# Half of a hybrid encoder layer's feed-forward by Strassen's seven products, its second matrix in three chunks

## The chip, the cores and the metric

The kernel runs on one core of one Trainium2 chip. A core has engines that run their own instruction queues side by side: TensorE (PE in the profile; PEld is its weight load) multiplies matrices into the accumulators (PSUM, eight banks), VectorE (DVE) and ScalarE (ACT) work on elements, SyncE (SP) issues most transfers. Semaphores hold an instruction until its data is there or its buffer is free; an engine's queue is in order, so an instruction that waits holds up all behind it.

The metric is the device time of one execution, in microseconds (us). Before the change it is 1327.59 us, the median of three runs (1327.44 to 1327.77).

## The reference, cut to what matters

Input is 512 tokens of 1024 features. 16 learned tokens are put in front (528 in all), and one layer follows: a feed-forward, a mixer of three branches (Fourier, short convolution, gated DeltaNet), and a second feed-forward. In front of each stands a norm, behind each another norm and the residual; the 16 tokens are dropped at the end. Everything is float32. The change is in both feed-forwards:

```python
def swiglu(x, wi, wo):
    a, b = jnp.split(x @ wi, 2, axis=-1)
    return (jax.nn.silu(a) * b) @ wo
...
h = h + 0.5 * rmsnorm(swiglu(rmsnorm(h, n[0]), ffn1_wi[l], ffn1_wo[l]), n[1])
```

`wi` is 1024 x 5632 and `wo` 2816 x 1024. In tiles of 128, x has 8 (`KD`), and the gated product 22 (`KF`). Tile m of a and tile m of b, columns m and 22 + m of `wi`, are the "tile pair" m.

## The kernel before, in words

**Layout.** Features lie on the 128 partitions and tokens on the free axis. The first feed-forward and the mixer's projections run over all 528 tokens, in two halves of 264 (`ALLC`), since a PSUM bank holds 512 numbers a partition; the second one over the 512 real tokens, whose halves of 256 fit one bank together (`REAL`, "joined").

**Numbers.** TensorE multiplies in float32r, which keeps 12 significant bits of an operand. So each operand is split into a high part h (a cast on ScalarE) and a low part l (a subtraction on VectorE), and each product is three passes: h x h, h x l, l x h. `mm` (the matmuls are issued on L137) does these three passes for one k. `load` fetches a tile of weights (1024 numbers a partition, 512 KB) on SP's queue to a staging tile `ws` (two buffers), casts it to `wh` (L219) and subtracts to `wl` (L220; three buffers each). `split` does the same for activations (L224, L225). `unit` is load, then `mm` over the 8 k: one tile of the first matrix.

**Order.** The order on TensorE is the order of the program. On the other engines a list scheduler sets it at build time, by priority (the place in the program) among what is ready; `load` is put 150 instructions ahead. Small side work of the norms and the mixer is put between the products by `side`, `tick` and `drain`.

**A feed-forward (`ffn`).** x has the gain of the norm in it, but not the root of the mean square: the first units run before this root (`rx`) is known. The three first tiles (a0, b0, a1) are begun in `start` or `edge`, three more follow, and meanwhile `xstat` has worked out `rx` (its last instructions are reciprocals on VectorE, L276). From then on each pair is: two units; each evicted from PSUM by VectorE with a multiplication by `rx` (`scaled`, L504); silu on ScalarE (L530); the product on VectorE (L526); and the split to tile m of `gh` and `gl`, which hold all 22 gated tiles. Then the second matrix: for each of the 8 output tiles, 22 k, whose weights come in three loads of 8, 8 and 6 tiles; `evict_y` copies the result to `ya`, squares it and adds up the squares for the norm.

**The edge.** The last output tile is left to the next stage (`tail`). `edge` does it half by half of the tokens (`part`), so that the norm, the residual and the next x of the first half go on while TensorE does the second half, and then begins the next stage's first three tiles. `finish` does the same at the end of the kernel, and writes the output.

Of the kernel before, what the change touches and what calls it, by code (L numbers as in the profile page):

```python
# [29 lines left out]
AHEAD = 150  # L30
XW = 5.0
# [23 lines left out]
# columns of the packed constants  # L55
# [45 lines left out]
class Cols:  # L101
    """Token columns of a stage, in two halves; joined: both fit one PSUM bank."""
# [17 lines left out]
class Tensor:  # L120
    """The tensor engine's instructions, with a sum of their length that orders the side work."""
# [22 lines left out]
class K:  # L144
# [43 lines left out]
    # side work goes between the large products; it yields how far on its next part goes  # L188
# [22 lines left out]
    # weights: staged as stored, then split into two parts of 12 significand bits  # L211
# [93 lines left out]
    def evict_y(self, ya, m, ps, gain=None, table=KD - 2):  # L305
        """ps: (half, what the products of tile m gave for it)"""
        y, acc = ya
        ACT, V = self.nc.scalar, self.nc.vector
        for i, p in ps:
            w = acc[i].shape[1]  # L310
            if gain is None:
                ACT.copy(y[i][:, m, :w], p)
            else:
                ACT.activation(y[i][:, m, :w], p, AF.Copy, scale=self.gains[:, gain, m:m + 1])
            if m == 0:
                ACT.activation(acc[i], p, AF.Square)
            else:
                sq = self.t(self.tp, "sy", [P, HN], F32, 1)[:, :w]
                ACT.activation(sq, p, AF.Square)  # L319
                V.tensor_tensor(acc[i], acc[i], sq, op=ALU.add)  # L320
        if m == table:
# [12 lines left out]
    def start(self, xT, gpre, srcs):  # L334
        """the first norm and tiles: everything arrives in the order of need"""
# [28 lines left out]
        # warm-up products while the first loads arrive  # L364
# [10 lines left out]
    def edge(self, C, hT, ya, gpost, gpre, tail, switch, nxt):  # L375
# [18 lines left out]
        tiles, tx, tc = tail()  # L394
        for t in tiles:
            self.evict_y(ya, t[0], [(0, self.part(t, tx, tc[0], W))], table=tiles[0][0] - 1)
# [12 lines left out]
        for t in tiles:  # L409
            self.evict_y(ya, t[0], [(1, self.part(t, tx, tc[1], W, lambda: next(e, None)))], table=-1)  # L410
# [20 lines left out]
    def finish(self, hT, ya, tail, out):  # L431
        """the last norm and residual; the second half of the tokens goes by tokens"""
# [5 lines left out]
        (tile,), tx, tc = tail()  # L438
        last = tile[0]
# [8 lines left out]
        self.evict_y(ya, last, [(0, self.part(tile, tx, tc[0], W))], 5, -1)  # L448
# [36 lines left out]
        p = self.part(tile, tx, tc[1], W, lambda: next(e, None))  # L485
# [3 lines left out]
        ACT.activation(sq[:, :W], p, AF.Square)  # L489
        ACT.activation(y[1][:, last, :W], p, AF.Copy, scale=self.gains[:, 5, last:last + 1])  # L490
# [20 lines left out]
    def open_ffn(self):  # L511
        ctx = ExitStack()
        gp = ctx.enter_context(self.tc.tile_pool(name=self.uid("gp"), bufs=1))
        self.gp = gp
        self.t3 = lambda: self.t(gp, "t3", [P, 530], F32, 3)
        return ctx

    def ffn(self, pre, wi, wo, C, gain=None):
        nc = self.nc
        x, os = pre  # L520
        gh = self.t(self.gp, "gh", [P, KF, L], F32R)
        gl = self.t(self.gp, "gl", [P, KF, L], F32R)
        u = C.u

        def pair(m, a, b):
            nc.vector.tensor_tensor(a[:, u], a[:, u], b[:, u], op=ALU.mult)  # L526
            self.split(gh[:, m, u], gl[:, m, u], a[:, u])

        def silu(a):
            nc.scalar.activation(a[:, u], a[:, u], AF.Silu)  # L530

        y = self.ytile().rearrange("p k c -> p (k c)")
        a, b, a1 = (y[:, i * L:(i + 1) * L] for i in range(3))
# [4 lines left out]
        for t in (a, b):  # L538
            nc.vector.tensor_tensor(t[:, u], t[:, u], self.rx[:, u], op=ALU.mult)
        silu(a)  # L540
        pair(0, a, b)
        nc.vector.tensor_tensor(a1[:, u], a1[:, u], self.rx[:, u], op=ALU.mult)
        silu(a1)
        b = self.t3()
        self.scaled(b, o)
        pair(1, a1, b)
        for m in range(2, KF):
            a = self.t3()
            self.scaled(a, o2 if m == 2 else self.unit(wi[m], x, C))
            silu(a)  # L550
            b = self.t3()
            self.scaled(b, o3 if m == 2 else self.unit(wi[KF + m], x, C))
            pair(m, a, b)
        ya = self.start_y(C)
        chunks = [(k0, min(8, KF - k0)) for k0 in range(0, KF, 8)]
        g = (gh, gl)
        for m in range(KD - 1):
            o = self.outs(C)
            for k0, n in chunks:
                w = self.load(wo[m][:, k0:k0 + n], n)  # L560
                for k in range(n):
                    self.mm(o.full, w, g, k, k0 + k, k0 + k == 0, k0 + k == KF - 1)
            self.evict_y(ya, m, [(i, p) for i, (p, _) in enumerate(o.half)], gain)

        def tail():
            ws = [(self.load(wo[KD - 1][:, k0:k0 + n], n), n, k0) for k0, n in chunks]
            return [(KD - 1, [(w, k, k0 + k) for w, n, k0 in ws for k in range(n)])], g, C.halves
        return ya, tail

# [18 lines left out]
    def mixer(self, pre, hT):  # L588
# [100 lines left out]
        def tail():  # L689
            ws = [(m, self.load(A["wout"][m])) for m in range(KD - NT, KD)]  # L690
            return [(m, [(w, k, k) for k in range(KD)]) for m, w in ws], (mh, ml), CS.halves
# [39 lines left out]
    def fold(self, q, o, fh, fl):  # L731
# [13 lines left out]
        def fold():  # L745
# [18 lines left out]
            # token L - k for k = 1 .. L/2 - 1  # L764
# [30 lines left out]
    # per-token scalars of both directions, [token, head, direction, tile]; tile 4: meta tokens  # L795
# [6 lines left out]
    def ab(self, ab):  # L802
# [23 lines left out]
        # softplus(a) = max(a, 0) + 2 atanh(e / (2 + e)), e = exp(-|a|)  # L826
# [5 lines left out]
        # beta = 1 / (1 + exp(-x))  # L832
# [50 lines left out]
    # short conv and silu of one head's q, k or v  # L883
# [8 lines left out]
    # token-major copies and l2norm  # L892
# [38 lines left out]
    # both heads' k: l2norm, token-major and back  # L931
# [41 lines left out]
    def rsqrt(self, dst, src, scale=1.0):  # L973
        """1 / sqrt(src * scale + eps) of a few columns: a first value from the exponent, then Newton's steps"""
# [11 lines left out]
    # chunk matrices and the scan of a pair of heads, both directions  # L986
    def dn_core(self, st, slack):
# [6 lines left out]
        # [token, head * 2 + direction, tile]  # L994
# [11 lines left out]
        # exponents gc_i - gc_j, masked  # L1006
# [36 lines left out]
        # inverses of the 32 x 32 diagonal blocks, one block a partition  # L1043
# [55 lines left out]
        # the blocks beside the diagonal  # L1099
# [25 lines left out]
        # scan  # L1125
# [80 lines left out]
    # gated norm of one head's output, back to channel-major, in place  # L1206
# [30 lines left out]
def body(tc, A):  # L1237
    nc = tc.nc
    with ExitStack() as ctx:
# [15 lines left out]
        ya, tail = k.ffn(pre, wi, wo, ALLC)  # L1255
# [14 lines left out]
        ya, tail = k.ffn(pre, wi, wo, REAL, 5)  # L1270
# [55 lines left out]
```

## Time and profile before

| | |
|---|---|
| median of three runs | 1327.59 us |
| the profiled execution: its span, from the first to the last instruction | 1325.0 us |
| TensorE: matmuls / weight loads, busy | 1311.5 us (99%) / 1159.8 us (88%) |
| VectorE / ScalarE, busy | 741.3 us (56%) / 492.3 us (37%) |
| first matrix of the first feed-forward, tile pair 2 on | about 37 to 266 us |
| its second matrix | 266 to 395 us |
| mixer, from the first to the second edge | 395 to 940 us |
| first matrix of the second feed-forward, tile pair 2 on, to the end of its second matrix | about 974 to 1319 us |
| read from HBM, written | 116.42 MB, 5.28 MB |

"Busy" is the time in which an engine has an instruction in work. Matmuls are pipelined: one of 264 columns is shown as 0.28 us long while the next one starts 0.12 us later, so what a stage costs is read from the distance of starts. A line such as `L137 PE MATMUL pb<-x,wh 128*128 128x264 f32` names the line of the code, the engine, the operation, output and inputs by tile name, the shape of the weights and of the moving side. In the windows, "x" stands before the number of instructions.

### The profile page before, as it was taken

What the parts mean: (1) busy time and instruction counts of PE and PEld (TensorE: products, weight loads), DVE (VectorE), ACT (ScalarE), POOL (GpSimd) and SP (SyncE); (2) the same over time, 40 slices, a digit from 0 to 9 for tenths busy, and PEclk for the clock granted to TensorE, in tenths of its full rate; (3) what the DMA queues carried; (4) which work ended last, traced back from release to release, by engine and by line L of the source; (5) the groups of instructions that cost most, each with busy time, mean ns of one, the idle gap of its engine ahead of it and who ended that gap; (6) DMA issues with size and microseconds to landing.
All of it is one profiled execution on the core that took longest, in us unless ns stands there. A gap on an engine that the chain in (4) does not pass through costs nothing.

```text
span 1325.0 us, 20942 instructions
## 1 busy us (share of the span) xinstructions
PE 1311.5 (99%) x8575; PEld 1159.8 (88%) x8575; DVE 741.3 (56%) x1524; ACT 492.3 (37%) x911; POOL 4.7 (0%) x12
## 2 busy tenths in 40 slices
PE   9999999999999999999999999999999999999998
PEld 9999999999999988778987777888978888888887
DVE  6644444422239888758788578564774444442223
ACT  7322222222235452344633434334552222222222
POOL 0000000000000000000000000000000000000000
PEclk9999999999999999999999999999999999999999
DMA  6322323333225222322221222235133332333332
GB/s 196 96 83 93 95 81 96 91 84 94 88 85 189 85 72 89 107 70 70 75 65 60 70 64 66 87 102 175 49 112 95 95 96 96 95 92 95 96 90 74
DMA packets 49844, 123.05 MB, mean 93 GB/s; under 512 B 13388, under 2 KB 17612, under 8 KB 49748
## 3 DMA queue, kind: packets, MB, share of 16 engines
q1 hardware_dynamic: 44660, 120.14, 29.2%
q10 hardware_dynamic: 5088, 1.57, 0.5%
q8 instruction: 67, 1.10, 0.3%
q14 instruction: 29, 0.24, 0.1%
HBM read 116.42 MB, written 5.28 MB: 92 GB/s over the span
## 4 chain that ended last, share of the span: by engine, by line
PE 95%; DVE 2%; ACT 1%; DMA 0%; SPq 0%; issue 0%; DVEq 0%; ACTq 0%
PE pb L137 86%; PE pd L137 8%; PE pd L141 1%; DVE s L386 1%; DVE x L391 1%; DVE wl L220 0%; DVE h L388 0%; ACT wh L219 0%; DMA h<-in_xT 0%; ACT O L1170 0%; DVE acc L288 0%; DVE x L499 0%; PE pb L141 0%; SPq L352 0%; ACT vp L1179 0%
## 5 line engine op out<-in xcount | busy, mean ns | idle before, releaser
L137 PE MATMUL pb<-x,wh 128*128 128x264 f32 (+3 forms) x3296 | 720.5, 325 | 3.5 <-DVE x L391 1.4
L137 PEld LDWEIGHTS pb<-x,wh 128*128 128x128 f32 x3296 | 513.8, 188 | 59.8 <-issue 4.6
L137 PE MATMUL pb<-x,wl 128*128 128x264 f32 (+3 forms) x1648 | 450.2, 323 | 1.1 <-DVE wl L220 1.0
L219 ACT CAST wh<-ws 128x1024 fp32r<-128x1024 f32 (+2 forms) x222 | 219.2, 988 | 613.3 <-PE pb L137 589.0
L220 DVE TENSOR_TENSOR wl<-ws,wh 128x1024 fp32r<-128x1024 f32 (+2 forms) x222 | 253.8, 1144 | 197.4 <-ACT wh L219 196.8
L137 PEld LDWEIGHTS pb<-x,wl 128*128 128x128 f32 x1648 | 276.5, 188 | 26.8 <-DVE wl L220 1.9
L504 DVE TENSOR_TENSOR t<-pb,rx 128x264 f32<-128x264 f32 (+2 forms) x144 | 67.7, 499 | 228.8 <-PE pb L137 228.8
L137 PE MATMUL pb<-gh,wh 128*128 128x264 f32 (+2 forms) x550 | 149.0, 316 | 0.0
L137 PE MATMUL pb<-gh,wl 128*128 128x264 f32 (+2 forms) x550 | 148.0, 315 | 0.0
L137 PE MATMUL pb<-gl,wh 128*128 128x264 f32 (+2 forms) x550 | 147.6, 314 | 0.0
L137 PEld LDWEIGHTS pb<-gl,wh 128*128 128x128 f32 x550 | 93.2, 188 | 6.9
L137 PEld LDWEIGHTS pb<-gh,wh 128*128 128x128 f32 x550 | 93.2, 188 | 6.5
L137 PEld LDWEIGHTS pb<-gh,wl 128*128 128x128 f32 x550 | 93.1, 188 | 6.6
L137 PE MATMUL pb<-y,wh 128*128 128x512 f32 x192 | 61.7, 402 | 0.0
L137 PEld LDWEIGHTS pb<-y,wh 128*128 128x128 f32 x192 | 34.4, 188 | 8.5 <-issue 2.2
L137 PE MATMUL pb<-y,wl 128*128 128x512 f32 x96 | 37.5, 391 | 0.0
L224 ACT CAST gh<-t 128x528 fp32r<-128x528 f32 (+1 forms) x40 | 25.1, 628 | 31.1 <-DVE t L526 31.1
L700 DVE TENSOR_TENSOR t<-pb,rx 128x512 f32<-128x512 f32 x24 | 16.6, 690 | 32.0 <-PE pb L137 32.0
L137 PE MATMUL pd<-x,wh 128*128 128x264 f32 (+2 forms) x176 | 33.3, 294 | 0.0
L1179 ACT ACTIVATE vp<-pd,be 64x128 f32<-64x128 f32 x64 | 23.2, 363 | 21.1 <-PE pd L137 19.8
L320 DVE TENSOR_TENSOR acc<-acc,sy 128x256 f32<-128x256 f32 (+1 forms) x41 | 17.4, 424 | 24.0 <-ACT sy L319 24.0
L526 DVE TENSOR_TENSOR t<-t,t 128x528 f32<-128x528 f32 (+1 forms) x40 | 28.0, 699 | 3.8
(261 smaller groups left out, 1113.1 us busy)
## 6 DMA issues: line engine op xcount, KB each, us to landing
ws<-in_wi SPq DMA_DIRECT2D x85, 512.0 KB, 3.5
ws<-in_wo SPq DMA_DIRECT2D x32, 512.0 KB, 3.4
ws<-in_win SPq DMA_DIRECT2D x32, 512.0 KB, 3.5
ws<-in_wg SPq DMA_DIRECT2D x24, 512.0 KB, 3.4
ws<-in_wo SPq DMA_DIRECT2D x16, 384.0 KB, 3.2
ws<-in_wout SPq DMA_DIRECT2D x8, 512.0 KB, 3.4
keep<-h SPq DMA_DIRECT2D x1, 2048.0 KB, 7.9
ws<-in_wsc SPq DMA_DIRECT2D x8, 256.0 KB, 2.7
```

The lines of the kernel that those rows point to most:

```text
L137: return self.e.matmul(out, lhsT, rhs, **kw)
L141: return self.e.transpose(*a)
L219: nc.scalar.copy(h[:, :nk], st[:, :nk])
L220: nc.vector.tensor_tensor(l[:, :nk], st[:, :nk], h[:, :nk].bitcast(F32), op=ALU.subtract)
L224: self.nc.scalar.copy(h, src)
L320: V.tensor_tensor(acc[i], acc[i], sq, op=ALU.add)
L386: V.scalar_tensor_tensor(t, ya[0][i][:, k, :W], self.gains[:, gpost, k:k + 1], r[:, c], op0=ALU.mult, op1=ALU.mult)
L391: V.scalar_tensor_tensor(x[1][:, k, c], hT[:, k, c], g, x[0][:, k, c].bitcast(F32), op0=ALU.mult, op1=ALU.subtract)
L504: self.nc.vector.tensor_tensor(dst[:, c.start + off:c.stop + off], p, self.rx[:, c], op=ALU.mult)
L526: nc.vector.tensor_tensor(a[:, u], a[:, u], b[:, u], op=ALU.mult)
L700: nc.vector.tensor_tensor(g, o.full[0][0], self.rx[:, NM:], op=ALU.mult)
L1179: ACT.activation(v1[X, hd], b[X, hd * P:(hd + 1) * P], AF.Copy, scale=beta[X, hd, t:t + 1])
```

## The change: what it does

**Seven products.** Write the pair m as a product of 2 x 2 blocks: x is cut by token half (i) and by its first and last four k tiles (j) to A_ij; the weights are cut by those k and by a or b. Strassen's scheme (in the variant with shared sums) gets the four results from seven products of half blocks in place of eight. Each product is 4 k x 3 passes over one token half. Pairs 4 to 21, 18 of 22, go this way; pairs 0 to 3 go as before.

`seven` (once in a stage, when `rx` is known) makes the normed x in `xn`, 16 instructions on VectorE, and the sums and high and low parts that products 1, 5 and 2 need; `rest`, called after pair 4's product 2, those for 6, 7, 3 and 4. `pair_load` fetches both weight tiles of a pair in four quarters, adds quarters (four additions of 512 columns on VectorE), and splits three tiles of 1024 and one of 512, 150 instructions ahead like `load`.

**Sums in PSUM.** Products are added up in the banks. Product 1 goes to bank b0; ScalarE copies b0 to b1; product 2 is added to b0, whose sum is a for the first half; 6 is added to b1; ScalarE copies b1 to b2; 7 and then 4 are added to b2; 3 to b1. Product 5 has a bank of its own and is copied out (`p5`). VectorE adds or subtracts `p5` when it evicts b2 after 7 and b1 after 3. b1 changes between two banks from pair to pair; there is one b2.

**Order of a pair on TensorE**: 1 of the new pair, 7 and 3 of the one before, 5 (new), 4 (before), 2 (new), 6 (new).

**Chunks.** `gh` and `gl` hold 8 gated tiles in place of 22. Pairs 0 to 5, then their part of the second matrix for all 8 output tiles; pairs 6 to 13, and their part; pairs 14 to 21, and theirs. ScalarE copies the first partial result to `ya`, VectorE adds the others. At a chunk's end the last pair's products 7, 3 and 4 are put between the first rows of the second matrix. In the last chunk three output tiles, not one, are left to `tail`, each with 8 k.

The diff, cut to its core:

```diff
+    def seven(self, hT, C, gpre):
...
+        for k in range(KD):
+            for i, c in enumerate(C.halves):
+                V.scalar_tensor_tensor(xn[i][:, k, :W], hT[:, k, c], self.gains[:, gpre, k:k + 1], self.rx[:, c],
+                                       op0=ALU.mult, op1=ALU.mult)
+        A11, A12 = xn[0][:, 0:4, :W], xn[0][:, 4:8, :W]
+        A21, A22 = xn[1][:, 0:4, :W], xn[1][:, 4:8, :W]
...
+        put(1, h3[:, 0, :, :W], l3[:, 0, :, :W], A11)
+        s5 = stage()
+        V.tensor_tensor(s5, A21, A22, op=ALU.subtract)
+        put(5, h3[:, 1, :, :W], l3[:, 1, :, :W], s5)
+        put(2, h3[:, 2, :, :W], l3[:, 2, :, :W], A12)
+
+        def rest():
...
+            V.scalar_tensor_tensor(s6, s5, -1.0, A11, op0=ALU.mult, op1=ALU.subtract)
+            put(6, h4[:, 0], l4[:, 0], s6)
...
+            V.tensor_tensor(s7, A11, A21, op=ALU.add)
+            put(7, h4[:, 1], l4[:, 1], s7)
...
+            V.scalar_tensor_tensor(s3, A12, -1.0, s6, op0=ALU.mult, op1=ALU.subtract)
+            put(3, h4[:, 2], l4[:, 2], s3)
+            ACT.mul(h4[:, 3], A22, -1.0)
+            V.scalar_tensor_tensor(l4[:, 3], A22, -1.0, h4[:, 3].bitcast(F32), op0=ALU.mult, op1=ALU.subtract)
...
+    def pair_load(self, w1, w2):
...
+        with self.tc.high_priority(AHEAD2):
+            fa, fb, fc = (self.t(self.gp, "wf", [P, KD, P], F32, 4) for _ in range(3))
+            fd = self.t(self.wp, "ws", [P, KD, P], F32, 2)
+            lo, hi = slice(0, 4), slice(4, 8)
+            nc.sync.dma_start(fa[:, lo], w1[:, lo])
+            nc.sync.dma_start(fd[:, hi], w2[:, lo])
+            nc.sync.dma_start(fb[:, lo], w1[:, hi])
+            nc.sync.dma_start(fc[:, hi], w2[:, hi])
...
+            V.tensor_tensor(fa[:, hi], fa[:, lo], fd[:, hi], op=ALU.add)
+            put(fa, 1, 5)
+            V.tensor_tensor(fb[:, hi], fa[:, hi], fc[:, hi], op=ALU.add)
+            put(fb, 2, 6)
+            V.tensor_tensor(fc[:, lo], fd[:, hi], fc[:, hi], op=ALU.add)
+            put(fc, 7, 3)
+            V.tensor_tensor(fd[:, lo], fb[:, hi], fb[:, lo], op=ALU.add)
+            put(fd, 4, None, 4, "w4", self.gp, 1)
...
+        def product(n, st, bank, start):
+            (wh, wl), (xh, xl) = st.w[n], X[n]
+            for k in range(4):
+                for i, (p, q) in enumerate(((wh, xh), (wh, xl), (wl, xh))):
+                    T.matmul(bank, p[:, k], q[:, k], start=start and k == 0 and i == 0, stop=k == 3 and i == 2,
+                             skip_group_check=True)
...
+        def begin(m):
...
+            st.b0, st.b1, st.b2 = self.big()[:, :W], seeds[0][count % 2], seeds[1][0]
...
+            product(1, st, st.b0, True)
+            ACT.copy(st.b1, st.b0)
...
+        def six(st):
+            product(6, st, st.b1, False)
+            ACT.copy(st.b2, st.b1)
+
+        def seven(st):
+            product(7, st, st.b2, False)
+            V.tensor_tensor(st.ev[:, 1, W:2 * W], st.b2, st.p5, op=ALU.add)
+            product(3, st, st.b1, False)
+            V.scalar_tensor_tensor(st.ev[:, 1, :W], st.b1, -1.0, st.p5, op0=ALU.mult, op1=ALU.subtract)
+
+        def four(st, g, m):
+            product(4, st, st.b2, False)
+            ACT.activation(st.ev[:, 0, W:2 * W], st.b2, AF.Silu, scale=-1.0)
+            pair(g, m, st.ev[:, 0, :2 * W], st.ev[:, 1, :2 * W])
...
+                nxt = begin(m)
+                if st:
+                    seven(st)
+                five(nxt)
+                if st:
+                    four(st, gc, st.m - k0)
+                two(nxt)
+                if m == 4:
+                    rest()
+                six(nxt)
+                st = nxt
```

In `evict_y` and `finish`, an addition on VectorE of the sum so far stands in front of the square for the last chunk's tiles.

More of the change, by code (lines that the diff above doesn't have):

```diff
@@ L310, in evict_y @@
             w = acc[i].shape[1]
-            if gain is None:
+            if more:
+                V.tensor_tensor(y[i][:, m, :w], y[i][:, m, :w], p, op=ALU.add)
+                p = y[i][:, m, :w]
+            elif gain is None:
                 ACT.copy(y[i][:, m, :w], p)
@@ L320, in evict_y @@
                 V.tensor_tensor(acc[i], acc[i], sq, op=ALU.add)
+            if more and gain is not None:
+                ACT.activation(p, p, AF.Copy, scale=self.gains[:, gain, m:m + 1])
         if m == table:
@@ L409, in edge @@
         for t in tiles:
[L410 removed]
+            self.evict_y(ya, t[0], [(1, self.part(t, tx, tc[1], W, lambda: next(e, None)))], table=-1, more=more)
         for k in range(3, KD):
@@ L437, in finish @@
         y, acc = ya
-        (tile,), tx, tc = tail()
-        last = tile[0]
+        tiles, tx, tc, more = tail()
+        last = tiles[-1][0]
         outA = out[:, :KD * W].rearrange("p (k c) -> p k c", k=KD)
@@ L447, in finish @@
         yT = []
-        self.evict_y(ya, last, [(0, self.part(tile, tx, tc[0], W))], 5, -1)
+        for t in tiles:
+            self.evict_y(ya, t[0], [(0, self.part(t, tx, tc[0], W))], 5, -1, more)
         bs = []
@@ L484, in finish @@
         e = early()
-        p = self.part(tile, tx, tc[1], W, lambda: next(e, None))
+        for t in tiles[:-1]:
+            self.evict_y(ya, t[0], [(1, self.part(t, tx, tc[1], W, lambda: next(e, None)))], 5, -1, more)
+        p = self.part(tiles[-1], tx, tc[1], W, lambda: next(e, None))
         for _ in e:
@@ L488, in finish @@
         sq = self.t(self.tp, "sy", [P, HN], F32, 1)
-        ACT.activation(sq[:, :W], p, AF.Square)
-        ACT.activation(y[1][:, last, :W], p, AF.Copy, scale=self.gains[:, 5, last:last + 1])
+        z = y[1][:, last, :W]
+        V.tensor_tensor(z, z, p, op=ALU.add)
+        ACT.activation(sq[:, :W], z, AF.Square)
+        ACT.activation(z, z, AF.Copy, scale=self.gains[:, 5, last:last + 1])
         for t in range(2):
@@ L520, in ffn, with gtiles, pair @@
+    def ffn(self, pre, wi, wo, C, hT, gpre, gain=None):
+        nc = self.nc
+        V, ACT, T = nc.vector, nc.scalar, self.T
         x, os = pre
-        gh = self.t(self.gp, "gh", [P, KF, L], F32R)
-        gl = self.t(self.gp, "gl", [P, KF, L], F32R)
         u = C.u
-        def pair(m, a, b):
-            nc.vector.tensor_tensor(a[:, u], a[:, u], b[:, u], op=ALU.mult)
-            self.split(gh[:, m, u], gl[:, m, u], a[:, u])
+        W = C.halves[0].stop - C.halves[0].start
+        chunks = [range(0, 6), range(6, 14), range(14, KF)]
+        def gtiles():
+            return tuple(self.t(self.gp, n, [P, KD, L], F32R) for n in ("gh", "gl"))
+        def pair(g, m, a, b):
+            V.tensor_tensor(a, a, b, op=ALU.mult)
+            self.split(g[0][:, m, u], g[1][:, m, u], a)
@@ L547, in ffn @@
[L547 to L563, printed above, removed]
+        self.scaled(b1, o)
@@ new lines, in ffn @@
+        pair(g, 1, a1[:, u], b1[:, u])
+        e = self.ev()
+        self.scaled(e[:, 0], o2)
+        silu(e[:, 0])
+        self.scaled(e[:, 1], o3)
+        pair(g, 2, e[:, 0, u], e[:, 1, u])
+        X, rest = self.seven(hT, C, gpre)
+        e = self.ev()
+        self.scaled(e[:, 0], self.unit(wi[3], x, C))
+        silu(e[:, 0])
+        self.scaled(e[:, 1], self.unit(wi[KF + 3], x, C))
+        pair(g, 3, e[:, 0, u], e[:, 1, u])
+        seeded = [self.dnp()[:, :W] for _ in range(3)]
@@ new lines, in five, with two @@
+        def five(st):
+            b4 = self.big()[:, :W]
+            product(5, st, b4, True)
+            st.p5 = self.t(self.gp, "p5", [P, HN], F32, 2)[:, :W]
+            ACT.copy(st.p5, b4)
+        def two(st):
+            product(2, st, st.b0, False)
+            ACT.activation(st.ev[:, 0, :W], st.b0, AF.Silu)
+        def six(st):
[6 more added lines that the diff above has]
+            V.scalar_tensor_tensor(st.ev[:, 1, :W], st.b1, -1.0, st.p5, op0=ALU.mult, op1=ALU.subtract)
@@ new lines, in four, with leave, ks, evict @@
+        def four(st, g, m):
+            product(4, st, st.b2, False)
+            ACT.activation(st.ev[:, 0, W:2 * W], st.b2, AF.Silu, scale=-1.0)
+            pair(g, m, st.ev[:, 0, :2 * W], st.ev[:, 1, :2 * W])
+        ya = None
+        for ci, ms in enumerate(chunks):
+            final = ci == len(chunks) - 1
+            gc, k0, n = g, ms.start, len(ms)
+            def leave(st):
+                seven(st)
+                four(st, gc, st.m - k0)
+            st = None
+            for m in ms:
+                if m < 4:
+                    continue
+                nxt = begin(m)
+                if st:
+                    seven(st)
+                five(nxt)
+                if st:
+                    four(st, gc, st.m - k0)
+                two(nxt)
[3 more added lines that the diff above has]
+                st = nxt
+            if ya is None:
+                ya = self.start_y(C)
+            ahead = []
+            for m in range(KD - 3 if final else KD):
+                o, w = self.outs(C), self.load(wo[m][:, k0:k0 + n], n)
+                def ks(r, o=o, w=w):
+                    for k in r:
+                        self.mm(o.full, w, gc, k, k, k == 0, k == n - 1)
+                def evict(m=m, o=o):
+                    ps = [(i, p) for i, (p, _) in enumerate(o.half)]
+                    if final:
+                        return self.evict_y(ya, m, ps, gain, more=True)
+                    for i, p in ps:
+                        y = ya[0][i][:, m, :W]
+                        if ci:
+                            V.tensor_tensor(y, y, p, op=ALU.add)
+                        else:
+                            ACT.copy(y, p)
+                if m < 2:
+                    ks(range(n - 1))
+                    ahead.append((ks, evict))
+                    if m == 0:
+                        leave(st)
+                    else:
+                        for f, e in ahead:
+                            f([n - 1])
+                            e()
+                else:
+                    ks(range(n))
+                    evict()
+            if not final:
+                g = gtiles()
```

80 lines of the change are left out of this document (59 added, 21 removed).

## The prediction

> **What bounds the kernel now.** I read the page first, then the chain that ended last, then the windows by stage, then the timeline of single engines.
>
> ```profile
> span 1325.0 us, 20942 instructions
> ...
> PE 1311.5 (99%) x8575; PEld 1159.8 (88%) x8575; DVE 741.3 (56%) x1524; ACT 492.3 (37%) x911; POOL 4.7 (0%) x12
> ```
> ```profile
> 42.77 345.15 PE pb L137 x2829
> ...
> 979.99 327.57 PE pb L137 x1455
> ```
> TensorE is busy for 99% of the span. The two lines of the chain are the two feed-forward stages: each is one unbroken piece of matmuls of L137, 345 and 328 us long, with nothing else in the chain. There a matmul taken out is time taken out, as long as the other engines keep up. How much they have to spare is in the windows, one inside each first-matrix loop (columns: length, then busy time of PE, PEld, DVE, ACT, POOL, granted clock, DMA share, GB/s):
>
> ```profile
> 66.00:150.00 84.00, 84.00 (x689) 84.00 (x688) 38.11 (x60) 24.02 (x29) 0.00 (x0) 1.00 0.29 88
> ...
> 1012.00:1100.00 88.00, 88.00 (x381) 71.34 (x380) 40.31 (x48) 26.22 (x32) 0.00 (x0) 1.00 0.30 94
> ```
> VectorE works 45% of this time, ScalarE 29%, DMA 30%, the clock is full. So VectorE is next in line, with a little over half of its time free.
>
> **What is saved on TensorE.** A unit (one tile of the first matrix) ends where VectorE starts to evict it:
>
> ```profile
> 54.43 0.77 DVE L504 TENSOR_TENSOR t<-pb,rx 128x264 f32<-128x264 f32 x2 [3.64 <-PE pb L137]
> ...
> 60.30 0.77 DVE L504 TENSOR_TENSOR t<-pb,rx 128x264 f32<-128x264 f32 x2 [2.54 <-PE pb L137]
> ```
> ```profile
> 985.59 0.69 DVE L504 TENSOR_TENSOR t<-pb,rx 128x512 f32<-128x512 f32 x1 [1.12 <-PE pb L137]
> ...
> 991.15 0.69 DVE L504 TENSOR_TENSOR t<-pb,rx 128x512 f32<-128x512 f32 x1 [3.43 <-PE pb L137]
> ```
> The first feed-forward does a unit in 5.87 us, for 8 k x 3 passes x 2 halves = 48 matmuls of 264 columns, 0.1223 us each. The second needs 5.56 us for 24 matmuls of 512 columns, 0.2317 us each. With the change (P1 to P7 below are its seven products, by the numbers of the code) the moving side has 256 columns there, each matmul with its own weight load. The end of the mixer has such a row of matmuls:
>
> ```profile
> 934.99 0.28 PE L137 MATMUL pb<-mh,wl 128*128 128x256 f32 x1
> ...
> 939.98 0.28 PE L137 MATMUL pb<-mh,wl 128*128 128x256 f32 x1
> ```
> Between these two starts lie 42 matmuls (14 k x 3), so 0.119 us each. A pair was 96 matmuls of 264 or 48 of 512 columns; it becomes 7 products x 4 k x 3 passes = 84 of 264 or 256. First: 11.74 to 84 x 0.1223 = 10.27, 1.47 saved. Second: 11.12 to 84 x 0.119 = 10.00, 1.12 saved. Times 18 pairs: 26.4 + 20.2 = 46.6 us. The second matrix keeps its matmuls; its three chunks only order them differently.
>
> The Trainium skill speaks against the second half of this: its page "TensorE: Matmul & The Clock Gate", section "Back-to-back issue gap", gives 131 ns a matmul of 512 columns and 81 ns of 128 in a stream with weight loads. An estimate from these two figures, on a straight line, is 98 ns at 256 columns, so 48 x 131 ns = 6.3 us would become 84 x 98 ns = 8.2 us and the second stage would lose 35 us. The rows above say 232 and 119 ns, so I give this no weight.
>
> **What it costs VectorE in the steady state.** Short instructions overlap a little, so I take distances between starts in dense stretches:
>
> ```profile
> 390.52 1.23 DVE L220 TENSOR_TENSOR wl<-ws,wh 128x1024 fp32r<-128x1024 f32 x1 [1.71 <-ACT wh L219]
> 391.67 0.89 DVE L386 SCALAR_TENSOR_TENSOR s<-y,gains,r 128x264 f32<-128x264 f32 x2
> 392.48 0.77 DVE L388 TENSOR_TENSOR h<-h,s 128x264 f32<-128x264 f32 x2
> 393.17 0.49 DVE L386 SCALAR_TENSOR_TENSOR s<-y,gains,r 128x264 f32<-128x264 f32 x1
> ```
> ```profile
> 976.89 1.28 DVE L504 TENSOR_TENSOR t<-pb,rx 128x512 f32<-128x512 f32 x2
> 978.09 0.68 DVE L526 TENSOR_TENSOR y<-y 128x512 f32<-128x512 f32 x1
> 978.69 0.68 DVE L526 TENSOR_TENSOR y<-y,t 128x512 f32<-128x512 f32 x1
> ```
> That gives 1.15 us for 1024 columns, 0.405 for a scalar_tensor_tensor of 264, 0.345 for a tensor_tensor of 264, and 0.60 for 512 (0.62 for 528). A pair now has four adds of weight quarters (2.4), low parts of three tiles of 1024 and one of 512 (4.05), the two evictions of P7 and P3 (0.345 + 0.405), the product and its low part (1.24): 8.4 us of 10.27 or 10.00, 82 to 84%. It fits, if the queue rarely stands still. ScalarE gets about six of ten.
>
> ```profile
> 37.77 1.04 ACT L219 CAST wh<-ws 128x1024 fp32r<-128x1024 f32 x1
> 38.71 0.64 ACT L530 ACTIVATE y<-y 128x528 f32<-128x528 f32 x1
> ```
> ```profile
> L312 ACT COPY y<-pb 128x264 f32<-128x264 f32 x16 | 6.0, 377 | 4.1 <-PE pb L137 4.1
> ```
> The tightest new wait is the copy of bank b1 to b2 after P6. P7 stands behind it with only P1 of the next pair between, 12 x 0.1223 = 1.47 us (1.43 in the second stage). No row shows a copy from PSUM to PSUM; the nearest one, PSUM to SBUF, is 0.377. P6 also frees the weight tile of products 2 and 6, and the cast into it, which has the higher priority, may go first: 0.94 + 0.377 and about 0.1 of handing over is 1.42 us. That just fits. If a second cast (0.6) stood ahead too, P7 would wait 0.6. Two other windows are wider: tile (1,5) is free after P5, with P4, P2, P6 (4.4 us) to do cast and low part (2.1); the others have five products. Below nothing isn't possible, TensorE has no slack left to gain. I take 0.05 a pair, 2 us in all, between 0 and 0.25 (9 us).
>
> Weights come as before, 1 MB a pair, in four transfers of 256 KB on SP's queue instead of two of 512:
>
> ```profile
> ws<-in_wsc SPq DMA_DIRECT2D x8, 256.0 KB, 2.7
> ```
> With four buffers for three staging tiles, the last quarter of the next pair is issued only when this pair's second tile is done with, about the time of P7, and lands 2.7 us later; its weights are due some 10 us after. The transfers behind it on the queue are due later still. No cost.
>
> **What it costs at the start of each stage.** The Strassen operands of x need the norm rx, so none of it can be done earlier, and all of it is VectorE's:
>
> ```profile
> 32.82 3.47 DVE L276 RECIPROCAL rx<-rx 128x264 f32<-128x264 f32 x2 [0.57 <-ACT rx L275]
> ```
> ```profile
> 42.61 0.65 PE L137 MATMUL pb<-x,wh 128*128 128x264 f32 x4
> ```
> ```profile
> 970.55 3.36 DVE L276 RECIPROCAL rx<-rx 128x256 f32<-128x256 f32 x2
> ```
> ```profile
> 979.83 0.63 PE L137 MATMUL pb<-x,wh 128*128 128x512 f32 x2
> ```
> rx is there at 36.3; tile 3's first unit starts at 42.61. Without waits tile 3 ends at 54.35, and eight products (1, 5, 2, 6 of pair 4, 1 of pair 5, 7 and 3 of pair 4, 5 of pair 5) later, at 66.1, P4 of pair 4 starts. Before that VectorE has: tiles 0 to 2 (12 operations of 0.62 and 0.69) 7.65; tile 3's weights 2 x 1.15; 16 normalisations of 264 columns, 6.48; eleven passes over 4 x 264 columns in seven() and rest(), 1.19 each, 13.05; tile 3's eviction 2.62; pair 4's weights 6.45; pair 5's adds and first low part 3.55; one eviction 0.35. Together 42.45, so 78.7: TensorE waits 12.6 us. The same list with 512 and 256 columns is 41.3 us from 973.9, to 1015.2, against 979.83 + 11.12 + 8 x 1.428 = 1002.4: 12.8 us. Together 25.4. If VectorE took things strictly in the order of need, three adds and tile 3's product could come later, 9.6 each (19). If the chains of difference, cast and low part leave it idle three times for a cast (0.94 each), 15.7 each (31). After pair 5 TensorE turns to the second matrix, 8 tiles of 36 matmuls (18 of double width in the second stage), where VectorE has little to do, so the debt isn't carried on.
>
> **Elsewhere.** The second matrix has three evictions a tile instead of one, VectorE or ScalarE under TensorE's 36 or 48 matmuls of a tile: hidden. At a chunk's end the last pair's P7, P3, P4 lie between rows of the second matrix that don't need them, and its gated tile is wanted only 3.7 us or more after P4: hidden. The tails go by three tiles of 8 k instead of one of 22, the same matmuls. An add of 0.345 per tile and half comes in front of the square; at the first edge, where VectorE is dense, I take 1.0, and at the very end 0.5: 1.5 (0.5 to 2.5).
>
> Sum: 46.6 - 25.4 - 2 - 1.5 = 17.7 us. The profiled execution has a span of 1325.0, 2.6 below the median of 1327.59; I take what lies around the span as unchanged. 1327.6 - 17.7 = 1310. Bounds: 46.6 - 19 - 0.5 = 27, 1300; 46.6 - 31 - 9 - 2.5 = 4, 1323.5.
>
> **The rivals.**
> *VectorE's queue binds in every pair* (slower). The queue is in order, and each low part needs ScalarE's cast first:
>
> ```profile
> DVE wl L220 <- ACT wh L219: 196.8, 111, 5.0
> ```
> It waits for casts now, 1.8 us at a time. If three of a pair's five low parts wait out a cast of 0.94 with nothing else let past, its 8.4 us become 11.2: 0.93 x 18 + 1.2 x 18 = 38 us of stalls, 1327.6 - 46.6 + 25.4 + 1.5 + 38 = 1346. It decides from a stall of 20/36 = 0.56 us a pair, that is 2.4 us of idle VectorE. For it: 84% load. Against: there are always adds to fill in, and these waits now occur where VectorE has nothing else.
>
> *The start is hidden after all*: VectorE's passes overlap more and come in the order of need, and TensorE waits 6 us in each stage: 46.6 - 12 - 1.5 and up to 2 less, 1294 to 1297. Against: the list has nothing in it that TensorE can do without.
>
> *The clock drops in the waits.* TensorE's last matmul ends at 1319.0:
>
> ```profile
> 1319.00:1321.00 2.00, 0.01 (x1) 0.00 (x0) 1.94 (x5) 0.04 (x1) 0.00 (x0) 1.00 0.10 39
> 1321.00:1325.00 4.00, 0.00 (x0) 0.00 (x0) 0.88 (x2) 0.00 (x0) 0.00 (x0) 0.74 0.64 243
> ```
> A mean of 0.74 is full clock for 1.9 us, then half: the drop comes some 3.9 us after the last work. The longest wait in my list is that of P6 of pair 4, for 3.5 us. If it is longer and the three products after it run at half speed, 3 x 1.47 is lost in each stage, at most 9 us: 1319. The Trainium skill ("TensorE: Matmul & The Clock Gate", "Part 1: The HAM clock gate") has half rate after an idle window of 3.4 us; the trace agrees within half a microsecond.
>
> *The matmuls aren't cheaper than I think*, because weights bind at 256 columns: PEld's 88% speaks for it, the row of 0.119 with a load each against it. No saving in the second stage: 1330.
>
> **How the numbers follow.** Forecast 0.66, queue 0.13, clock 0.08, hidden start 0.07, weights 0.06. A measurement can tell about 0.2% (2.7 us) from no change. The range 1296 to 1327 takes in forecast and clock and half of the hidden start, and leaves out the queue and most of the weights' case: 0.8. Faster: 0.66 + 0.08 + 0.07, less 0.05 for the forecast's upper end: 0.76. Same 0.06, slower 0.18.
>
> **What would show it.** Right: pairs every 10.3 and 10.0 us in the middle of a chunk with VectorE at 80 to 90%; waits of TensorE for VectorE right after tile 3, 10 to 15 us in each stage; nearly none later. Wrong: PE waits for ScalarE or VectorE in every pair, a pair period over 10.8 us, or no wait after tile 3.

## The result, and the profile after

| | before | after |
|---|---|---|
| median, beside each other (four runs each) | 1327.68 us | 1345.13 us (1344.24 to 1347.99) |
| the profiled execution / its span | 1327.8 / 1325.0 us | 1347.99 / 1345.8 us |
| TensorE busy | 1311.5 us | 1289.4 us |

The ratio is 1.0135 [1.0121, 1.0149]: 17.4 us slower, where I forecast 17.7 us faster. The page of the changed kernel gives the contradiction at once: TensorE is busy for 22 us less in a span 21 us longer.

```profile
PE 1289.4 (96%) x9019; PEld 1166.1 (87%) x9019; DVE 933.0 (69%) x1822; ACT 607.8 (45%) x1155; POOL 4.7 (0%) x12
```

TensorE is idle for 43 us more than before, which must show as waits. The waits of TensorE, grouped by what ended them (total, times, longest):

```profile
PE pd L138 <- ACT pd L695: 11.3, 24, 1.0
PE pb L138 <- DVE ev L515: 10.1, 1, 10.1
...
PE pb L138 <- DVE l L226: 6.0, 2, 4.9
```

The first is a wait in nearly every pair, for ScalarE. (L695 is the copy of b1 to b2, L225 and L226 are `split`, L515 is `scaled`; all matmuls are L138.) The others are a few long ones, at the start of each stage.

**Every pair.** The chain between two pairs in the middle of the first stage (start, length, what):

```profile
285.82 3.17 PE pd L138 x24
...
293.37 1.35 PE pd L138 x11
...
294.78 1.05 ACT wh L225
295.83 0.53 ACT gh L225
296.36 0.29 ACT pd L695
...
296.69 3.17 PE pd L138 x24
```

P6 ends at 294.72. On ScalarE two casts of `split` come first, the weights' (1.05) and that of the gated tile (0.53), and only then the copy that P7 needs; P1, the only product between, is over after 1.45. From P7 to P7 it is 10.87 us in this stage; in the second, 10.66:

```profile
1092.65 3.12 PE pd L138 x24
...
1103.31 3.11 PE pd L138 x24
```

**The starts.** TensorE's waits there, from its timeline; in brackets the idle time before the instruction and what ended it. At 56.31 TensorE has done tile 3 and three short matmuls that seed the new banks. The last row of each stage is P4 of pair 4 (weights `w4h`):

```profile
55.78 0.53 PE L138 MATMUL pd<-h,wh 128*128 128x264 f32 x3
66.42 0.59 PE L138 MATMUL pb<-h,wh 128*128 128x264 f32 x1 [10.11 <-DVE ev L515]
...
76.52 0.59 PE L138 MATMUL pd<-x,wh 128*128 128x264 f32 x1 [2.79 <-ACT x L225]
77.87 0.59 PE L138 MATMUL pd<-x,wh 128*128 128x264 f32 x1 [0.77 <-DVE x L226]
86.22 0.39 PE L138 MATMUL pd<-x,wh 128*128 128x264 f32 x1 [1.32 <-DVE x L226]
...
89.11 0.41 PE L138 MATMUL pd<-x,w4h 128*128 128x264 f32 x2
...
1005.07 0.62 PE L138 MATMUL pd<-h,wh 128*128 128x256 f32 x3 [1.90 <-ACT h L225]
1010.68 0.58 PE L138 MATMUL pb<-l,wh 128*128 128x256 f32 x1 [4.88 <-DVE l L226]
1014.69 0.58 PE L138 MATMUL pb<-l,wh 128*128 128x256 f32 x1 [1.07 <-DVE l L226]
1022.53 0.58 PE L138 MATMUL pd<-x,wh 128*128 128x256 f32 x1 [3.43 <-ACT x L225]
1023.84 0.58 PE L138 MATMUL pd<-x,wh 128*128 128x256 f32 x1 [0.73 <-DVE x L226]
...
1032.86 0.40 PE L138 MATMUL pd<-x,w4h 128*128 128x256 f32 x2
```

In the first stage they add up to 15.0 us, in the second to 12.0. But P4 comes later than that: after tile 3's end at about 55.7 and eight products without a wait (11.7) it would have come at 67.4, so some 21.7 us are lost; in the second stage, counted in the same way, 18.4. The rest is in the granted clock (columns as in the prediction's windows; the clock stands before the last two):

```profile
58.00:59.00 1.00, 0.00 (x0) 0.00 (x0) 1.00 (x4) 0.43 (x1) 0.00 (x0) 0.87 0.00 0
...
67.00:72.00 5.00, 5.00 (x25) 5.00 (x24) 1.80 (x4) 1.55 (x4) 0.00 (x0) 0.50 0.00 0
72.00:73.00 1.00, 1.00 (x9) 1.00 (x8) 0.04 (x1) 1.00 (x2) 0.00 (x0) 0.80 0.00 0
...
75.00:76.00 1.00, 0.00 (x0) 0.00 (x0) 0.97 (x2) 0.61 (x1) 0.00 (x0) 0.91 0.52 182
...
82.00:83.00 1.00, 1.00 (x7) 1.00 (x7) 0.79 (x1) 0.00 (x0) 0.00 (x0) 0.68 0.08 16
...
1016.00:1018.00 2.00, 2.00 (x12) 2.00 (x12) 0.03 (x1) 0.77 (x1) 0.00 (x0) 0.53 0.00 0
...
1028.00:1030.00 2.00, 2.00 (x18) 2.00 (x17) 1.91 (x2) 1.03 (x2) 0.00 (x0) 0.97 0.12 17
```

A mean of 0.80 from 72 to 73 is half clock up to 72.4, then full. So after the wait of 10.1 us TensorE is at half clock for 6.0 us (66.42 to 72.4), and after that of 2.8 us for another 6.1 (76.52 to 82.6), of which it waits 0.8. Half of what is worked in them is lost, at most 3.0 and 2.7 us. 15.0 + 5.7 is the 21.7, but for 1.0, of which the matmuls that seed the banks take some 0.6. The second stage has two such stretches too, up to 1017.9 and 1028.1 (the last two rows); by the same working they lose 3.1 and 2.4.

Why VectorE freed the bank so late in the first stage stands in its own timeline:

```profile
58.85 1.26 DVE L226 TENSOR_TENSOR l<-y,h 128x1056 fp32r<-128x1056 f32 x1
...
64.12 0.69 DVE L602 TENSOR_TENSOR wf<-wf,wf 128x512 f32<-128x512 f32 x1
...
65.33 0.69 DVE L606 TENSOR_TENSOR ws<-wf 128x512 f32<-128x512 f32 x1
65.93 1.45 DVE L515 TENSOR_TENSOR ev<-pb,rx 128x264 f32<-128x264 f32 x4
...
72.96 1.23 DVE L226 TENSOR_TENSOR wl<-wf,wh 128x1024 fp32r<-128x1024 f32 x1 [3.36 <-ACT wh L225]
```

The four evictions of tile 3 (L515) begin at 65.93, after the low parts of the sums and three additions for pair 5 (`pair_load`; a fourth came at 62.35), which nobody needs yet. Its second unit was ready at 55.7, its first one a unit earlier. P1 of pair 4 needs one of those banks; it starts when the first eviction is done. Its own low part (58.85) was there at 60.1, so some 6 of the 10.1 us are the bank's, and the rest is VectorE's work on P1's operand. Later, at 69.6 to 72.96, VectorE stands idle for 3.4 us behind a cast whose weight buffer the slow TensorE still holds. In the second stage no bank is in question: there the 4.88 us ahead of P1's low-part matmul are a wait for that operand alone.

### The profile page after: what moved, and what is told of

It is laid out like the page before. It is cut to its first block, busy times and chain, and to the rows that moved or that the text cites. A ratio compares the mean times of both kernels' runs of the same rounds, so it can differ in the third digit from the quotient of the medians.

```text
span 1345.8 us, 22626 instructions
## 1 busy us (share of the span) xinstructions
PE 1289.4 (96%) x9019; PEld 1166.1 (87%) x9019; DVE 933.0 (69%) x1822; ACT 607.8 (45%) x1155; POOL 4.7 (0%) x12
## 4 chain that ended last, share of the span: by engine, by line
PE 85%; DVE 7%; ACT 5%; issue 2%; DMA 1%; SPq 0%; DVEq 0%; ACTq 0%
PE pb L138 61%; PE pd L138 23%; ACT wh L225 2%; DVE wl L226 1%; PE pd L142 1%; DMA wf<-in_wi 1%; ACT gh L225 1%; DVE y L545 1%; DVE wl L221 1%; ACT wh L220 1%; DVE x L397 1%; ACT pd L695 0%; DVE s L392 0%; DVE l L226 0%; DMA h<-in_xT 0%
## 5 line engine op out<-in xcount | busy, mean ns | idle before, releaser
L138 PE MATMUL pb<-x,wh 128*128 128x264 f32 (+3 forms) x1568 | 355.5, 331 | 5.9 <-DVE x L397 2.1
L138 PEld LDWEIGHTS pb<-x,wh 128*128 128x128 f32 x1568 | 247.4, 190 | 37.3 <-issue 4.6
L138 PE MATMUL pb<-x,wl 128*128 128x264 f32 (+3 forms) x784 | 220.3, 326 | 1.0 <-DVE wl L221 1.0
L138 PE MATMUL pd<-x,wh 128*128 128x264 f32 (+2 forms) x1040 | 199.1, 291 | 20.3 <-ACT pd L695 11.3
L221 DVE TENSOR_TENSOR wl<-ws,wh 128x1024 fp32r<-128x1024 f32 (+2 forms) x150 | 165.4, 1107 | 70.9 <-ACT wh L220 69.6
L225 ACT CAST wh<-wf 128x1024 fp32r<-128x1024 f32 x108 | 113.6, 1052 | 174.5 <-PE pd L138 112.5
L138 PEld LDWEIGHTS pd<-x,wh 128*128 128x128 f32 x1040 | 162.0, 191 | 28.1 <-ACT pd L695 16.2
L226 DVE TENSOR_TENSOR wl<-wf,wh 128x1024 fp32r<-128x1024 f32 x108 | 132.0, 1222 | 38.2 <-ACT wh L225 37.6
L138 PE MATMUL pb<-gh,wh 128*128 128x264 f32 (+2 forms) x552 | 150.5, 317 | 1.0 <-ACT y L751 1.0
L138 PE MATMUL pb<-gh,wl 128*128 128x264 f32 (+2 forms) x552 | 148.9, 315 | 0.0
L138 PE MATMUL pb<-gl,wh 128*128 128x264 f32 (+2 forms) x552 | 148.8, 314 | 0.0
L138 PEld LDWEIGHTS pb<-x,wl 128*128 128x128 f32 x784 | 134.2, 190 | 14.4 <-DVE wl L221 1.7
L138 PE MATMUL pd<-x,wl 128*128 128x264 f32 (+2 forms) x520 | 145.1, 287 | 0.0
L138 PE MATMUL pb<-h,wh 128*128 128x264 f32 (+1 forms) x432 | 125.3, 290 | 10.1 <-DVE ev L515 10.1
L138 PE MATMUL pb<-l,wh 128*128 128x264 f32 (+1 forms) x432 | 125.8, 291 | 6.0 <-DVE l L226 6.0
L138 PE MATMUL pb<-h,wl 128*128 128x264 f32 (+1 forms) x432 | 124.9, 289 | 0.0
L138 PEld LDWEIGHTS pb<-gh,wh 128*128 128x128 f32 x552 | 94.1, 188 | 8.1 <-ACT y L751 1.2
L138 PEld LDWEIGHTS pb<-gh,wl 128*128 128x128 f32 x552 | 93.8, 188 | 6.6
L138 PEld LDWEIGHTS pb<-gl,wh 128*128 128x128 f32 x552 | 93.6, 188 | 6.5
L138 PEld LDWEIGHTS pd<-x,wl 128*128 128x128 f32 x520 | 97.8, 191 | 0.3
L138 PEld LDWEIGHTS pb<-h,wh 128*128 128x128 f32 x432 | 84.9, 197 | 10.4 <-DVE ev L515 10.3
```

The source lines that it names most:

```text
L138: return self.e.matmul(out, lhsT, rhs, **kw)
L221: nc.vector.tensor_tensor(l[:, :nk], st[:, :nk], h[:, :nk].bitcast(F32), op=ALU.subtract)
L225: self.nc.scalar.copy(h, src)
L226: self.nc.vector.tensor_tensor(l, src, h.bitcast(F32), op=ALU.subtract)
```

## The experiments

Theories for the 35 us between forecast and result. A: the copy to b2 stands behind two casts, some 0.53 us a pair. B: at the start, tile 3's evictions free the banks too late. C: the clock's half pace makes each of those waits dearer. Against them: R1, my rival of the prediction, VectorE's list binds in every pair; and R3, the chunks and edges cost far more than the 1.5 us I gave them. All medians below are from runs beside the kernel before (1327.8 us for the first four, 1327.3 for the last three).

**The copy ahead of the casts.**

```diff
         def six(st):
             product(6, st, st.b1, False)
-            ACT.copy(st.b2, st.b1)
+            with self.tc.high_priority(400):
+                ACT.copy(st.b2, st.b1)
```

> The copy of bank b1 to b2 after product 6 is put ahead of the casts in ScalarE's queue; nothing else. Theory A (in every pair product 7 waits for this copy, which stands behind two casts of 1.05 and 0.62 us): the wait of 0.42 us before product 7 goes, pairs come every 10.3 us in the first and 10.0 us in the second stage instead of 10.88 and 10.66, some 30 pairs gain 0.6 each, 1345 becomes about 1327. Rival R1 (VectorE's queue binds in every pair, the copy only happens to be last): the wait moves to a low part or an addition, the period stays at 10.7 or more, 1342 to 1346.

Measured: 1330.77 us (1328.12 to 1333.58), 1.0024 [1.0014, 1.0033] of before: 14.4 us of the 17.4 are gone, though 3.8 less than I expected. ScalarE's timeline, and TensorE's chain at P7, in both stages:

```profile
288.76 1.05 ACT L225 CAST wh<-wf 128x1024 fp32r<-128x1024 f32 x1 [0.99 <-PE pd L138]
289.72 0.37 ACT L696 COPY pd<-pd 128x264 f32<-128x264 f32 x1
290.03 0.62 ACT L225 CAST gh<-ev 128x528 fp32r<-128x528 f32 x1
```
```profile
279.90 3.07 PE pd L138 x24
...
290.25 3.07 PE pd L138 x24
```
```profile
1092.46 3.03 PE pd L138 x24
...
1102.58 3.03 PE pd L138 x24
```

One cast ahead and not two, and the wait is gone from every pair: 10.35 us a pair in the first stage and 10.12 in the second, where it was 10.87 and 10.66. VectorE's work is the same, so R1 falls: its list did not bind. A is shown.

**Tile 3's evictions first.**

```diff
-        self.scaled(e[:, 0], self.unit(wi[3], x, C))
-        silu(e[:, 0])
-        self.scaled(e[:, 1], self.unit(wi[KF + 3], x, C))
-        pair(g, 3, e[:, 0, u], e[:, 1, u])
+        o, o2 = self.unit(wi[3], x, C), self.unit(wi[KF + 3], x, C)
+        with self.tc.high_priority(400):
+            self.scaled(e[:, 0], o)
+            silu(e[:, 0])
+            self.scaled(e[:, 1], o2)
+            pair(g, 3, e[:, 0, u], e[:, 1, u])
```

> The evictions of tile 3 are given priority on VectorE. Theory A for the start (product 1 of pair 4 waits for a bank that VectorE frees last, and the long gap lets the clock fall): product 1 starts some 4 us sooner, and with a shorter gap part of the half-speed time goes too; 3 to 10 us less in all, 1335 to 1342. Rival R2 (VectorE's sum of work sets the start, whatever its order): product 4 of pair 4 starts at the same time within 1 us, 1343 to 1346.

Measured: 1341.35 us (1339.74 to 1342.22), 1.0097 [1.0080, 1.0114]: 3.8 us better than the change as it was. TensorE's timeline:

```profile
61.19 0.58 PE L138 MATMUL pb<-h,wh 128*128 128x264 f32 x1 [4.63 <-DVE ev L515]
71.59 0.59 PE L138 MATMUL pd<-x,wh 128*128 128x264 f32 x1 [4.23 <-ACT x L225]
```

The first wait falls from 10.1 to 4.6 us, and the next one grows from 2.8 to 4.2. So B is true of the first wait, but part of it only moves: what VectorE puts off for the eviction (the operands of P6) is what is late next. From tile 3's end to P4 the first stage now takes 26.6 us instead of 33.3, so R2, by which that time doesn't depend on the order, falls there. In the second stage the waits of 1.90 and 4.88 us ahead of P1 stand as before, and it takes 31.0 instead of 29.9.

**TensorE kept busy in the waits.** The kernel adds useless matmuls of 128 columns, into a bank that nobody reads, before P1 and before P6 of pair 4; what it computes is unchanged.

```diff
+        warm = self.dnp()
+        def busy(n):
+            for _ in range(n):
+                T.matmul(warm[:, :P], self.ones, self.ones, start=True, stop=True)
+        busy(16 if C.joined else 22)
...
                 if m == 4:
                     rest()
+                    busy(8)
```

> Matmuls without use (on a constant, into a spare bank) fill TensorE's two longest waits at the start of each stage: 22 or 16 before product 1 of pair 4, 8 before its product 6. Theory C (the clock that falls in the wait costs by itself: about 11 us at half speed in each stage): the granted clock stays at 1.0 and 4 to 10 us go, 1335 to 1341. Rival R2 (VectorE's sum of work sets the start; slow products only fill the wait): the clock stays up and the time doesn't change by more than 2 us, 1343 to 1347.

Measured: 1338.37 us (1335.22 to 1340.65), 1.0075 [1.0057, 1.0094]: 6.8 us better, for matmuls that compute nothing. P1 of pair 4 in the first stage, and the windows:

```profile
61.72 0.39 PE L138 MATMUL pb<-h,wh 128*128 128x264 f32 x1 [2.25 <-DVE ev L515]
```
```profile
54.00:66.00 12.00, 9.75 (x83) 9.48 (x82) 11.92 (x18) 6.64 (x9) 0.00 (x0) 1.00 0.24 78
66.00:80.00 14.00, 9.26 (x56) 8.77 (x56) 12.74 (x12) 6.16 (x10) 0.00 (x0) 0.76 0.08 26
```

In the change as it was the same two windows had a clock of 0.70 and 0.62. The second wait (here 4.0 us, only part of it filled) still brings the clock down, which I had not expected. And the run does not show C by itself, since more than the clock has changed. P1 starts at 61.72 instead of 66.42, because VectorE begins tile 3's evictions at 61.24, ahead of the additions for pair 5; probably the added instructions shifted the priorities, which go by the place in the program. From tile 3's end to P4 it takes 28.9 us in the first stage and 28.2 in the second (33.3 and 29.9 in the change as it was). So part of the 6.8 us is B's, and how much stays open. What the slow clock costs beside a wait is shown by the last experiment.

**Strassen from pair 6 on.** If the starts lose because the list of VectorE is due too early, later is better. Pairs 4 and 5 go by two units, so only 16 of 22 pairs go by seven products; `rest` runs before them.

```diff
-        e = self.ev()
-        self.scaled(e[:, 0], self.unit(wi[3], x, C))
...
+        for m in range(3, 6):
+            e = self.ev()
+            self.scaled(e[:, 0], self.unit(wi[m], x, C))
+            silu(e[:, 0])
+            self.scaled(e[:, 1], self.unit(wi[KF + m], x, C))
+            pair(g, m, e[:, 0, u], e[:, 1, u])
+        rest()
...
-                if m < 4:
+                if m < 6:
```

> Pairs 4 and 5 go as before by two units each, so that the first chunk has no Strassen pair; 16 of 22 pairs by seven products, the operands of x are made beside tiles 3 to 5 and the first part of the second matrix. It gives up 2 x 1.47 + 2 x 1.12 = 5 us of saving. If the start of the stages costs what the trace shows (product 4 of pair 4 comes 21.7 and 18.4 us later than the matmuls ahead of it would need), 1345 - 40 + 5 = 1310, with up to 6 us more if the first tiles of the second matrix wait for VectorE. If the start's loss only moves to another place: 1335 to 1350.

Measured: 1316.88 us (1314.75 to 1318.70), 0.9914 [0.9900, 0.9929]: the first version faster than before, though 7 us short of the 1310 I expected, and just beyond the 6 us I had allowed for a wait at the second matrix. Its long wait at the start, and the window behind it:

```profile
PE pb L138 <- DVE ev L515: 4.4, 1, 4.4
```
```profile
59.00:65.00 6.00, 5.95 (x28) 5.98 (x29) 3.48 (x6) 1.27 (x2) 0.00 (x0) 0.54 0.39 134
```

A single start wait is left, again a bank that VectorE frees late, now ahead of an ordinary unit; 4.4 us and, with a mean clock of 0.54 in the six that follow, nearly 3 more. Those would be the 7 us; the last experiment takes the wait away.

**The chunks alone.** No Strassen: every pair by two units, but the second matrix in three chunks and tails of three tiles.

```diff
-        X, rest = self.seven(hT, C, gpre)
...
+        def two_units(m, k0):
+            e = self.ev()
+            self.scaled(e[:, 0], self.unit(wi[m], x, C))
+            silu(e[:, 0])
+            self.scaled(e[:, 1], self.unit(wi[KF + m], x, C))
+            pair(g, m - k0, e[:, 0, u], e[:, 1, u])
...
+            if ci:
+                for m in ms:
+                    two_units(m, k0)
```

> No Strassen products at all: every pair by two units, but the second matrix in three chunks and the tails of three tiles, as in the changed kernel. My own step (chunks and tails cost 1.5 us, 0.5 to 2.5): 1328 to 1330. Rival R3 (the chunks cost more, which would explain why the kernel with the copy first still isn't faster than the one before): 1333 or more.

Measured: 1334.28 us (1333.95 to 1335.99), 1.0053 [1.0038, 1.0068]: 7.0 us slower than before. Three points of its chain, of which the first and the third answer to the two lines of the chain of before:

```profile
46.14 13.95 PE pb L138 x114
...
430.68 5.06 PE pb L138 x42
...
985.43 37.07 PE pb L138 x160
```

and in the chain of before the row that answers to the second:

```profile
425.22 5.06 PE pb L137 x42
```

46.14 against 42.77 is 3.4 us at the kernel's own start; 430.68 against 425.22 is 5.5, so 2.1 more up to the mixer; 985.43 against 979.99 is 5.4, so the mixer costs nothing; and the span is 7.7 longer, so 2.3 lie in the second feed-forward and the end. What makes these two is not shown. Of the 3.4, 1.8 are a slower first load (6.0 us from issue to landing, 4.2 before), the rest slower matmuls right behind it. The load varies by execution: the last kernel below has 4.35, and is 0.2 behind at that point (42.96). So R3 is half right: 4.4 us belong to chunks and edges, and how much of the other 2.6 in the medians is the change's stays open.

**Both: from pair 6, and the copy first.** The edits of the first and fourth experiments together.

```diff
+            with self.tc.high_priority(400):
+                ACT.copy(st.b2, st.b1)
...
-                if m < 4:
+                if m < 6:
```

> Both edits: the copy first on ScalarE, and Strassen from pair 6 on. If the two losses are separate things they add up: 1327.8 - 10.9 from the one, and some 28 pairs at 0.55 = 15 from the other, 1301 to 1303. If the copy's wait only covered another one that stands behind it (R1 again): 1308 or more.

Measured: 1303.26 us (1302.41 to 1303.90), 0.9816 [0.9799, 0.9832]. The copy is worth about 13 us here (24.0 less 10.9, each against the kernel before beside it), 14.4 on the change as it was: the losses add up, one does not hide another. One wait is left of those in question:

```profile
59.55 1.28 PE L138 MATMUL pb<-x,wh 128*128 128x264 f32 x4 [4.40 <-DVE ev L515]
```

**And other banks for the units ahead.** The second unit of tiles 3 to 5 takes a bank of another pool, so that no unit waits for the eviction of one before:

```diff
-            self.scaled(e[:, 1], self.unit(wi[KF + m], x, C))
+            self.scaled(e[:, 1], self.unit(wi[KF + m], x, C, new=self.dnp))
```

> As the one before, and in tiles 3 to 5 the second unit of each pair goes to the other four banks, so that TensorE isn't held up by an eviction that VectorE does late (one wait of 4.4 us in the first stage, after which the clock is at half speed for some 5 us). If that wait and its clock are what is left at the start: 5 to 7 us less, 1295 to 1297. If VectorE's sum sets the start even so: no change.

Measured: 1295.88 us (1295.69 to 1296.55), 0.9762 [0.9748, 0.9777], 2.4% faster than before; 7.4 us better than the last. Only the wait of 4.4 us is taken away, so the slow clock behind it costs the other 3: that is C, shown at this place. The page, and TensorE's chain through the start of the first stage:

```profile
PE 1275.9 (99%) x8971; PEld 1153.0 (89%) x8971; DVE 915.7 (71%) x1802; ACT 597.7 (46%) x1131; POOL 4.7 (0%) x12
```
```profile
42.96 5.87 PE pb L138 x48
48.84 5.87 PE pd L138 x48
```

No wait is left at the starts (the longest of all are some 1.1 us), and units follow each other every 5.87 us, as in the kernel before. TensorE is at 99% again, with 36 us less to do.

## Why the prediction was wrong, point by point

**The saving on TensorE: right, 8% too high.** Forecast 10.27 and 10.00 us a pair; without waits (the copy-first kernel) 10.35 and 10.12, so 1.39 and 1.00 saved, 43.0 us in 18 pairs each where I had 46.6; the order of the pair, without waits, was right. Behind P7's first matmul the stream is some 0.1 us late, even where nothing is waited for; no row of before has such a place. The rival in which weights bind at 256 columns is refuted: the second stage's pairs went from 11.12 to 10.12 us. So is the estimate from the Trainium skill ("TensorE: Matmul & The Clock Gate", "Back-to-back issue gap") by which the second stage would lose: here the measurement decides.

**The steady state: failed.** "I take 0.05 a pair, 2 us in all." It was 0.53 a pair and 14.4 us. I had written the very case, a second cast ahead of the copy, with its price of 0.6, and reckoned with one cast because I saw only the weights' cast become free at that moment. The other, the gated tile's, was ready too: the product of the pair before is done just when P6 is. I should have listed ScalarE's whole queue around P6, as I did for VectorE, rather than the tightest instruction alone. With this step alone right the sum would have been 12.4 us longer, about 1322, and still faster; the largest miss is the next one.

**The start: failed, 25.4 us forecast, 40.1 measured.** The waits alone are 27.0 us, near the forecast, but in part by luck, since they are not the waits I had. What failed is "the longest wait in my list is that of P6 of pair 4, for 3.5 us", for which the prediction shows no working, and on which the clock stayed a rival with 0.08. P6 did wait 2.8 and 3.4 us, but more stood ahead of P1: 10.1 us in the first stage, 1.9 and 4.9 in the second. My list named tile 3's evictions ahead of pair 4's weights and pair 5's additions; in the first stage VectorE did them behind these. And it added up VectorE's work to the date of P4 alone, not to that of P1's operands. Four stretches at half clock followed, two a stage, and by their length made up some 11 of the other 13 us. Even the wait that I had counted was long enough: the clock had fallen after 2.8 us as after 10.1. That clock cost belongs in the sum as soon as a wait of some 3 us does.

**Chunks and edges: 1.5 us forecast, 4.4 to 7.0 measured**, 2.1 by the first edge and 2.3 by the second stage's end, the rest at the kernel's start. The term was too small; which instruction makes up the difference is open.

**The sum.** 43.0 saved, less 40.1, 14.4 and 7.0, is 18.5 us slower; measured 17.4 in the median, and 20.3 in the execution from whose profile the 40.1 is. For the last kernel: 16/18 of 43.0 is 38.2, less 7.0, 31.2 us faster; measured 31.4. With only the 4.4 that belong to chunks and edges it would be 33.8, so the sums are good to 2 or 3 us, not better.

**The rivals.** "VectorE's queue binds in every pair" gave 1346 and the result is 1345, but its mechanism is wrong: moving one copy on ScalarE removes the wait of each pair, and VectorE is not the bound in the middle of the second stage, where it works 73% of the time (7.8 us of a pair's 10.66; I had 8.4):

```profile
1060.00:1140.00 80.00, 77.80 (x584) 73.86 (x583) 58.48 (x80) 40.60 (x72) 0.00 (x0) 1.00 0.29 93
```

The number was hit by accident. "The start is hidden" is refuted for the change as it was, and comes true when the products begin two pairs later and the units ahead of them have banks of their own. "The clock drops in the waits" was true, and by the length of the stretches dearer than its price of at most 9.

**What would have shown it.** I had named "PE waits for ScalarE or VectorE in every pair, a pair period over 10.8 us" as the sign of a wrong forecast; the first stage had 10.87.

## What to carry to other kernels

When a change inserts a copy on the path between two matmuls, write down the whole queue of the engine that makes it, with everything that becomes ready in the same moment, not the copy's own time. Where a list of preparations is due before a stage can begin, begin it with work that doesn't need them (here two more pairs the old way cost 4.8 us of saving and gave back over 30), and look at which of the postponed instructions free a buffer that TensorE needs. A wait of TensorE of some 3 us or more cost 2 to 3 us more afterwards here.

## What the runs showed of the hardware

The clock doesn't fall at a fixed time after the last matmul. In the profile after it fell 2.4 us after (work until 56.31, half from 58.74) and 2.1 us after (73.7, then 75.82); before the change, at the end, some 3.9. In the kernel from pair 6 the wait of 4.4 us began at 54.65, and the clock was full until 57.68:

```profile
57.00:58.00 1.00, 0.00 (x0) 0.00 (x0) 1.00 (x2) 0.00 (x0) 0.00 (x0) 0.84 0.00 0
```

Nor is the way back fixed: 5.5 to 6.1 us from the first matmul on in the three cases above, 7.2 and 5.6 in the second stage. But the switches lie on a grid. Those of the rows above, at 58.74, 72.40, 75.82, 82.64, 1017.88 and 1028.12, are 4, 1, 2, 274 and 3 times 3.4133 us apart (935.24 / 274), to 0.02; those of the kernel from pair 6 (57.68 and 64.52), 2 times. In the three cases with a way back of 5.5 to 6.1 us the clock was full again at the end of the first whole step of the grid that TensorE worked through (68.99 to 72.40, 79.23 to 82.64, 61.10 to 64.52); the part of a step before it, in which work began, did not do. So what a wait costs depends on where in the grid it ends. How much idle time in a step brings the clock down, no run here shows. The Trainium skill ("TensorE: Matmul & The Clock Gate", "Part 1: The HAM clock gate") speaks of a free-running window of about 3.4 us in both directions. The trace agrees on that: the grid runs on through both stages. But a fall needs no wholly idle step: in the one before 58.74, TensorE worked until 56.31.

A copy from PSUM to PSUM of 264 columns took 0.37 us on ScalarE (the copy's row above), the same as the copy from PSUM to SBUF that I had taken for it.
